# Eight small copy-out tiles instead of six, and an earlier copy-out of the gates' chunk

## The chip, the cores and the metric

The kernel runs on one core of a Trainium2 chip. The metric is the device time of one execution in microseconds (us), the median of several runs. "PE" is the matrix engine, "PEld" its weight load, "DVE" the vector engine, "ACT" the scalar engine, "POOL" GpSimd and "SP" the engine that issues most of the transfers; SPq and POOLq are the instructions by which SP and POOL issue transfers.

## What is computed

One decoder layer on 256 tokens of width 4096, in float32. An RMS norm is followed by one input projection into thirteen groups of columns, by two attention mixers (a dilated one and a sparse one), by gated RMS norms and by an output projection. The part that matters here is the projection:

```python
h = _rmsnorm(x, norm_g[l])
proj = h @ w_in[l]
(q_a, k_a, v_a, z_a, q_b, kc, vc, ksl, vsl, kwn, vwn, z_b, g_b) = jnp.split(
    proj, _split_points(), axis=-1)
```

`q_a`, `k_a`, `v_a` and `q_b` are 2048 columns each, 16 chunks of 512 in all. `g_b` (48 columns) holds the gates of the sparse mixer; the kernel computes it in one chunk with the 256 columns of `vwn`, called `vg` here (304 columns).

## The kernel before, in words

Every operand of a matmul is a sum of a high and a low part in a rounded format (`h` and `l`): ACT rounds the high part, DVE subtracts it from the original and leaves the low part, and each product is three matmuls, h·h, h·l and l·h (`mm3`, L97 to L100). This preparation is called a split.

The program has three stages. In the first, five chunks of the projection are computed from 1 MB pieces of weights; the `vg` chunk is the last of them, and its two sums (one for each half of the tokens) stand in two PSUM banks named `acc`.

The second is the paired stage (`run_pairs`, L409 to L518). Its 16 chunks are taken two at a time: eight groups, in the order q0/q1, k0/k1, v0/v1, qb0/qb1, q2/q3 and so on. A group has 16 steps. A step takes a 2x2 arrangement of weight blocks (two k-tiles by two chunks) and the matching 2x2 arrangement of x blocks. In a **plain** step it does 8 products (24 matmuls), in a **fast** step 7 products (21 matmuls) on sums of blocks; nine steps of a group are fast (`FAST`), seven plain. Before its matmuls a step needs its split (`split_blocks`, L440): for a fast step ACT rounds the raw blocks (L444) and twice sums that DVE has made (L447, L450), while DVE does L445, L448, L449, then the low parts L451 and L452; for a plain step ACT does one rounding of 2048 columns and DVE one subtraction (L105 and L106 of `split_to`). The engines work in the order in which the code is written (`manual_schedule`).

Three operand buffers (`f0`, `f1`, `p`; tiles `bf` and `bp`) hold split operands, and three raw buffers (`bw`) hold loaded weights. `split_on(n)`, called after step n's matmuls, does the splits up to step n+3 whose operand buffer was last used by a step that is done. Each split ends with the load for three steps later (L437 and L438 on SP).

The eight PSUM banks collect eight partial sums, `p1` to `p7` and `e`. The fast steps write p1 to p7; the plain steps write p3, p2, p4 and e. After the last fast step p1, p7, p5 and p6 are final, after the last plain step p3, p2, p4 and e. In groups two to eight the last fast step is two steps before the end, in the first group (order `FIRST`) one step before it. `put_sums` (L462) copies each final bank with ACT into a tile `parts` (128x512, float32) and POOL writes it to the result in HBM: p1 with four plain transfers, the others with accumulating transfers into those of the four result blocks that they belong to (p7 2, p5 2, p6 3, p3, p2, p4 and e one each, 15 transfers in all). Transfers into the same result block follow each other, each waiting until the one before has landed. The `parts` tiles come from a ring of six (L465): the seventh copy of a group (p4) waits until the transfers out of p1's tile have landed, the eighth (e) until those out of p7's have. The next group writes the same eight banks, each as soon as it has been copied.

The copy-out of the last group's p3, p2, p4 and e is left to the third stage's beginning (`rest`), where ACT also rounds that stage's first weights. The third stage does the other projections, both mixers and the output projection.

At the beginning of the paired stage the code loads the weights of three steps, does the splits of steps 0, 1 and 2 (`split_on(-1)`, L485), and then calls `begin` (`begin_pairs`, L1120), which copies the two banks of `vg` out with ACT (`evict_away`, L545, tile `away`) and stores them with SP (L546). The banks of the paired stage are the same memory: step 0 can write the banks under `vg` only after these copies. The order of the first group's steps is plain, plain, fast, plain, fast, fast, plain ...

Of the kernel before, what the change touches and what calls it, by code (L numbers as in the profile page):

```python
# [11 lines left out]
F32 = mybir.dt.float32  # L12
# [6 lines left out]
P = 128  # L19
# [7 lines left out]
CW = 512  # L27
# [56 lines left out]
def hybrid_trunk(ctx: ExitStack, tc: tile.TileContext, a: dict):  # L84
# [9 lines left out]
    room = {}  # L94
# [7 lines left out]
    def split_to(h, l, src, scale=None):  # L102

        if scale is None:
            nc.scalar.activation(h, src, AF.Copy)  # L105
            nc.vector.tensor_sub(l, src, h.bitcast(F32))  # L106
        else:
            nc.scalar.activation(h, src, AF.Copy, scale=scale)
            nc.vector.scalar_tensor_tensor(l, src, scale, h.bitcast(F32), op0=OP.mult, op1=OP.subtract)
# [299 lines left out]
    def run_pairs(dcs, begin):  # L409
# [21 lines left out]
        def load(n):  # L431
            if n < N:
                d, i = steps[n]
                w, (g, half) = raw[n % LOADS], divmod(i, 2)
                ks = slice(2 * half, 2 * half + 2)
                c0, c1 = dcs[d][0]
                nc.sync.dma_start(w[:, B11 : B21 + 1], a["w_in"][c0, g][:, ks])  # L437
                nc.sync.dma_start(w[:, B12 : B22 + 1], a["w_in"][c1, g][:, ks])  # L438

        def split_blocks(n):  # L440
            w, t = raw[n % LOADS], sums_b
            h, l = hl[place[n]][:, 0], hl[place[n]][:, 1]
            if FAST[steps[n][1]]:
                nc.scalar.activation(h[:, :3], w[:, B22:], AF.Copy)  # L444
                nc.vector.tensor_tensor(t[:, T3 : T1 + 1], w[:, B22 : B11 + 1],  # L445
                                        w[:, B12 : B12 + 1].to_broadcast([P, 2, CW]), op=OP.subtract)
                nc.scalar.activation(h[:, 3:5], t[:, T3 : T1 + 1], AF.Copy)  # L447
                nc.vector.tensor_add(t[:, T2], w[:, B22], t[:, T1])  # L448
                nc.vector.tensor_sub(t[:, T4], w[:, B21], t[:, T2])  # L449
                nc.scalar.activation(h[:, 5:], t[:, T2:], AF.Copy)  # L450
                nc.vector.tensor_sub(l[:, :3], w[:, B22:], h[:, :3].bitcast(F32))  # L451
                nc.vector.tensor_sub(l[:, 3:], t, h[:, 3:].bitcast(F32))  # L452
            else:
                split_to(h[:, :4], l[:, :4], w)
            load(n + LOADS)
# [6 lines left out]
        def put_sums(d, ps, banks):  # L462
            dst = [scratch(dcs[d][1][c])[:, m] for c, m in ((0, 0), (1, 0), (0, 1), (1, 1))]
            for b in banks:
                t = room["parts"].tile([P, CW], F32, name="parts", tag="parts", bufs=6)  # L465
                nc.scalar.activation(t, ps[b], AF.Copy)
                for c in {"p1": (0, 1, 2, 3), "p5": (1, 3), "p6": (1, 2, 3), "p7": (2, 3),
                          "p2": (0,), "p3": (1,), "p4": (2,), "e": (3,)}[b]:
                    if b == "p1":
                        nc.gpsimd.dma_start(dst[c], t)  # L470
                    else:
                        nc.gpsimd.dma_start(dst[c], t, accum_op=OP.add)

        split = 0

        def split_on(n):

            nonlocal split
            while split < N and split <= n + 3 and prev[split] <= n:
                split_blocks(split)  # L480
                split += 1

        for n in range(LOADS):
            load(n)
        split_on(-1)  # L485
        begin()
        for n, (d, i) in enumerate(steps):
            if n % NKP == 0:
                ps = {b: room["banks"].tile([P, CW], F32, name=b) for b in BANKS} if d == 0 else dict(ps)
# [7 lines left out]
            if FAST[i]:  # L497
                s = lambda j: (sops[i][:, 0, j], sops[i][:, 1, j])
                e = not any(FAST[k] for _, k in steps[n + 1 : n - n % NKP + NKP])
                raws, sums = -B22, 3  # L500
                for bank, lhs, b in (
                    ("p1", block(i, 0, 0), raws + B11), ("p7", s(2), sums + T3), ("p5", s(0), sums + T1),
                    ("p6", s(1), sums + T2), ("p3", s(3), raws + B22), ("p2", block(i, 0, 1), raws + B21),
                    ("p4", block(i, 1, 1), sums + T4),
                ):
                    product(bank, lhs, b, e and bank in ("p1", "p5", "p6", "p7"))
                if e:
                    put_sums(d, ps, ("p1", "p7", "p5", "p6"))
            else:
                e = n % NKP == NKP - 1  # L510
                for bank, row, cols in (("p3", 0, (B12, B22)), ("p2", 0, (B11, B21)), ("p4", 1, (B11, B21)), ("e", 1, (B12, B22))):
                    for col, b in enumerate(cols):
                        product(bank, block(i, row, col), b, e and col == 1)
                if e and d == len(dcs) - 1:
                    return lambda: put_sums(d, ps, ("p3", "p2", "p4", "e"))
                if e:
                    put_sums(d, ps, ("p3", "p2", "p4", "e"))
# [12 lines left out]
    def scratch(key, width=CW):  # L530
        if key not in scr:
            scr[key] = dram.tile([P, NT, width], F32, name=f"scr_{key}")
        return scr[key]
# [598 lines left out]
    with tc.manual_schedule():  # L1132
        rest = run_pairs(dcs, begin_pairs)
# [85 lines left out]
```

## Time and profile before

| | us |
|---|---|
| median of 3 runs | 1724.02 (1720.05 to 1729.22) |
| the profiled execution, its own time | 1725.84 |
| its span, first to last instruction | 1724.1 |
| paired stage within it | 193.3 to 907.1 |
| PE busy | 1659.7 (96%) |
| DVE busy | 1243.6 (72%) |
| ACT busy | 959.4 (56%) |
| mean granted PE clock | 0.984 |

Rows of the timeline read: start, duration, engine, line and operation, out <- in, count, and in brackets the idle time of the engine before it and what ended that. Rows of the windows read: stretch, its length, and for each engine its busy time and in brackets its instructions, then granted clock as a share of full speed, DMA share and GB/s.

### The profile page before, as it was taken

What the parts mean: (1) busy time and instruction counts of PE and PEld (TensorE: products, weight loads), DVE (VectorE), ACT (ScalarE), POOL (GpSimd) and SP (SyncE); (2) the same over time, 40 slices, a digit from 0 to 9 for tenths busy, and PEclk for the clock granted to TensorE, in tenths of its full rate; (3) what the DMA queues carried; (4) which work ended last, traced back from release to release, by engine and by line L of the source; (5) the groups of instructions that cost most, each with busy time, mean ns of one, the idle gap of its engine ahead of it and who ended that gap; (6) DMA issues with size and microseconds to landing.
All of it is one profiled execution on the core that took longest, in us unless ns stands there. A gap on an engine that the chain in (4) does not pass through costs nothing.

```text
span 1724.1 us, 20835 instructions
## 1 busy us (share of the span) xinstructions
PE 1659.7 (96%) x7853; PEld 1359.1 (79%) x7853; DVE 1243.6 (72%) x1576; ACT 959.4 (56%) x1243; POOL 97.2 (6%) x129
## 2 busy tenths in 40 slices
PE   9999997999999998999998999999999999999997
PEld 6889875787878786878787778777888888888887
DVE  7496596979798887888876778887865655555553
ACT  6676464546465555555545677677654544444443
POOL 0000001011111111020211000000000000000000
PEclk9999998999999899999999999999999999999999
DMA  9875667878787868696969645543454466566554
GB/s 344 297 274 174 202 207 194 243 244 230 245 228 242 238 225 234 224 253 211 269 243 327 239 171 200 199 140 124 158 193 176 169 214 214 213 214 213 202 196 157
DMA packets 92661, 376.74 MB, mean 219 GB/s; under 512 B 10896, under 2 KB 12304, under 8 KB 73104
## 3 DMA queue, kind: packets, MB, share of 16 engines
q1 hardware_dynamic: 73152, 336.61, 55.6%
q0 software_dynamic: 15232, 31.46, 9.5%
q10 hardware_dynamic: 4176, 7.34, 1.3%
q8 instruction: 61, 1.00, 0.2%
q14 instruction: 40, 0.33, 0.1%
HBM read 335.48 MB, written 39.90 MB: 218 GB/s over the span
## 4 chain that ended last, share of the span: by engine, by line
PE 59%; DVE 9%; DMA 9%; issue 6%; ACT 4%; POOL 1%; ACTq 0%; SPq 0%; POOLq 0%; DVEq 0%
PE acc L100 11%; PE acc L99 11%; PE acc L98 11%; PE p L99 6%; PE p L100 5%; PE p L98 5%; DVE bf L452 2%; DMA scr_q<-parts 2%; DMA scr_qb<-parts 2%; DMA bw<-in_w_in 2%; DMA scr_k<-parts 2%; DVE bf L451 2%; DVE bt L445 1%; DMA scr_v<-parts 1%; DVE bt L448 1%
## 5 line engine op out<-in xcount | busy, mean ns | idle before, releaser
L106 DVE TENSOR_TENSOR wl<-w,wh 128x1024 fp32r<-128x1024 f32 (+2 forms) x306 | 365.1, 1194 | 274.4 <-ACT wh L105 273.8
L105 ACT ACTIVATE wh<-w 128x1024 fp32r<-128x1024 f32 (+2 forms) x306 | 316.4, 1035 | 297.0 <-PE acc L100 290.6
L98 PE MATMUL acc<-wh,xh 128*128 128x512 f32 (+2 forms) x768 | 292.5, 382 | 0.5 <-ACT wh L105 0.5
L99 PE MATMUL acc<-wl,xh 128*128 128x512 f32 (+2 forms) x768 | 291.1, 379 | 1.7 <-DVE wl L106 1.6
L100 PE MATMUL acc<-wh,xl 128*128 128x512 f32 (+2 forms) x768 | 291.2, 379 | 0.0
L98 PE MATMUL acc<-wh,yh 128*128 128x512 f32 (+1 forms) x512 | 192.8, 377 | 0.0
L100 PE MATMUL acc<-wh,yl 128*128 128x512 f32 (+1 forms) x512 | 192.5, 376 | 0.0
L99 PE MATMUL acc<-wl,yh 128*128 128x512 f32 (+1 forms) x512 | 192.4, 376 | 0.0
L99 PEld LDWEIGHTS acc<-wl,xh 128*128 128x128 f32 x768 | 144.9, 189 | 26.5 <-DVE wl L106 3.5
L452 DVE TENSOR_TENSOR bf<-bt,bf 128x2048 fp32r<-128x2048 f32 x72 | 164.5, 2285 | 0.8
L98 PEld LDWEIGHTS acc<-wh,xh 128*128 128x128 f32 x768 | 144.7, 189 | 25.4 <-ACT wh L105 2.3
L100 PEld LDWEIGHTS acc<-wh,xl 128*128 128x128 f32 x768 | 144.8, 189 | 24.2
L451 DVE TENSOR_TENSOR bf<-bw,bf 128x1536 fp32r<-128x1536 f32 x72 | 126.1, 1752 | 44.8 <-ACT bf L444 44.8
L106 DVE TENSOR_TENSOR bp<-bw,bp 128x2048 fp32r<-128x2048 f32 x48 | 109.9, 2289 | 62.0 <-ACT bp L105 62.0
L447 ACT ACTIVATE bf<-bt 128x1024 fp32r<-128x1024 f32 x72 | 76.4, 1061 | 140.4 <-DVE bt L445 140.4
L99 PE MATMUL p<-bf,sum 128*128 128x512 f32 x288 | 117.8, 409 | 13.3 <-DVE bf L452 13.2
L105 ACT ACTIVATE bp<-bw 128x2048 fp32r<-128x2048 f32 x48 | 91.6, 1908 | 62.2 <-PE e L100 43.1
L98 PE MATMUL p<-bp,xh 128*128 128x512 f32 x288 | 113.4, 394 | 6.7 <-ACT bp L105 6.7
L444 ACT ACTIVATE bf<-bw 128x1536 fp32r<-128x1536 f32 x72 | 106.6, 1481 | 21.2 <-DMA bw<-in_w_in 19.8
L100 PE MATMUL p<-bf,sum 128*128 128x512 f32 x288 | 114.7, 398 | 0.0
L99 PE MATMUL p<-bp,xh 128*128 128x512 f32 x288 | 113.2, 393 | 1.5 <-DVE bp L106 1.5
L98 PE MATMUL p<-bf,sum 128*128 128x512 f32 x288 | 114.5, 398 | 0.0
(279 smaller groups left out, 2928.4 us busy)
## 6 DMA issues: line engine op xcount, KB each, us to landing
bw<-in_w_in SPq DMA_DIRECT2D x256, 512.0 KB, 5.2
w<-in_w_in SPq DMA_DIRECT2D x76, 1024.0 KB, 4.9
w<-in_w_out SPq DMA_DIRECT2D x64, 1024.0 KB, 4.8
scr_q<-parts POOLq DMA_DIRECT2D x30, 256.0 KB, 7.3
scr_k<-parts POOLq DMA_DIRECT2D x30, 256.0 KB, 8.1
scr_v<-parts POOLq DMA_DIRECT2D x30, 256.0 KB, 8.0
scr_qb<-parts POOLq DMA_DIRECT2D x30, 256.0 KB, 8.7
w<-in_w_vg SPq DMA_DIRECT2D x8, 608.0 KB, 3.7
```

Of the source, the lines that this page charges most:

```text
L98: nc.tensor.matmul(out, lh, rh, start=start, stop=False)
L99: nc.tensor.matmul(out, lh, rl, start=False, stop=False)
L100: nc.tensor.matmul(out, ll, rh, start=False, stop=stop)
L105: nc.scalar.activation(h, src, AF.Copy)
L106: nc.vector.tensor_sub(l, src, h.bitcast(F32))
L444: nc.scalar.activation(h[:, :3], w[:, B22:], AF.Copy)
L445: nc.vector.tensor_tensor(t[:, T3 : T1 + 1], w[:, B22 : B11 + 1], w[:, B12 : B12 + 1].to_broadcast([P, 2, CW]), op=OP.subtract)
L447: nc.scalar.activation(h[:, 3:5], t[:, T3 : T1 + 1], AF.Copy)
L448: nc.vector.tensor_add(t[:, T2], w[:, B22], t[:, T1])
L451: nc.vector.tensor_sub(l[:, :3], w[:, B22:], h[:, :3].bitcast(F32))
L452: nc.vector.tensor_sub(l[:, 3:], t, h[:, 3:].bitcast(F32))
```

## The change

```diff
-                t = room["parts"].tile([P, CW], F32, name="parts", tag="parts", bufs=6)
+                t = room["parts"].tile([P, CW], F32, name="parts", tag="parts", bufs=8)
...
-        split_on(-1)
+        for split in range(2):
+            split_blocks(split)
+        split = 2
         begin()
+        split_on(-1)
```

The ring of copy-out tiles has eight places instead of six, one for each bank of a group. At the beginning of the paired stage the splits of steps 0 and 1 are done first, then `begin`, then the split of step 2. The changed program has three lines more from there on, so that L545 is L548 in it.

ACT at the beginning of the paired stage: `bf` and `bp` are the operand buffers, `away` the copies of the `vg` banks (`acc`). The piece shows the instructions before, with -, and now, with +.

```order
 L105 ACTIVATE bf_1811<-bw_1813 128x2048 [waits DMAHW4_49,DMAHW3_49]
 L105 ACTIVATE bp<-bw_1814 128x2048 [waits DMAHW6_49,DMAHW5_49,DVE_49]
-L444 ACTIVATE bf_1817<-bw_1815 128x1536 [waits DMAHW7_49,DMAHW0_49,PE_49]
+L548 ACTIVATE away<-acc 128x304 [waits PE_49] x2
+L444 ACTIVATE bf_1817<-bw_1815 128x1536 [waits DMAHW7_49,DMAHW0_49]
 L447 ACTIVATE bf_1817<-bt 128x1024 [waits DVE_49]
 L450 ACTIVATE bf_1817<-bt 128x1024 [waits DVE_49]
-L545 ACTIVATE away<-acc 128x304 x2
```

The two copies have moved ahead of the three roundings of step 2's split; they wait for PE (the last matmuls of `vg`) by themselves now.

ACT at the end of the first group: the copies of p3, p2, p4 and e into `parts`, and the next split, of a plain step. DMASW are the semaphores of POOL's transfers.

```order
 L466 ACTIVATE parts<-p_1863 128x512 [waits PE_49]
 L466 ACTIVATE parts<-p_1862 128x512 [waits PE_49]
-L466 ACTIVATE parts<-p_1860 128x512 [waits DMASW1_49,DMASW2_49,DMASW0_49,DMASW3_49,PE_49,Activation_49]
-L466 ACTIVATE parts<-e 128x512 [waits DMASW4_49,DMASW5_49,PE_49,Activation_49]
-L105 ACTIVATE bp<-bw_1815 128x2048 [waits DMAHW7_49,DMAHW6_49]
+L466 ACTIVATE parts<-p_1860 128x512 [waits PE_49]
+L466 ACTIVATE parts<-e 128x512 [waits PE_49]
+L105 ACTIVATE bp<-bw_1815 128x2048 [waits DMAHW7_49,DMAHW6_49,Activation_49]
```

Nothing has moved here; the seventh and the eighth copy no longer wait for transfers.

ACT at the end of the second group, the same four copies and the next split, of a fast step:

```order
-L466 ACTIVATE parts<-p_1863 128x512 [waits DMASW5_49,PE_49]
-L466 ACTIVATE parts<-p_1862 128x512 [waits DMASW6_49,PE_49]
-L466 ACTIVATE parts<-p_1860 128x512 [waits DMASW1_49,DMASW2_49,DMASW0_49,DMASW7_49,PE_49,Activation_49]
-L466 ACTIVATE parts<-e 128x512 [waits DMASW3_49,DMASW4_49,PE_49,Activation_49]
-L444 ACTIVATE bf_1817<-bw_1814 128x1536 [waits DMAHW1_49,DMAHW0_49]
+L466 ACTIVATE parts<-p_1863 128x512 [waits DMASW3_49,PE_49]
+L466 ACTIVATE parts<-p_1862 128x512 [waits DMASW4_49,PE_49]
+L466 ACTIVATE parts<-p_1860 128x512 [waits DMASW5_49,PE_49]
+L466 ACTIVATE parts<-e 128x512 [waits DMASW6_49,PE_49]
+L444 ACTIVATE bf_1817<-bw_1814 128x1536 [waits DMAHW1_49,DMAHW0_49,Activation_49]
```

Here too the order stays; each copy waits for the transfers out of the same bank's tile of the group before, no longer for transfers of its own group. PE's, DVE's and POOL's instructions stand in the same order as before in the whole program. On SP the store of `vg` stands one load earlier, ahead of the load for step 5 that ends step 2's split.

More of the change, by code (lines that the diff above doesn't have):

```diff
@@ L484, in run_pairs @@
             load(n)
+        for split in range(2):
+            split_blocks(split)
+        split = 2
+        begin()
         split_on(-1)
-        begin()
         for n, (d, i) in enumerate(steps):
```

## The prediction

> **What bounds the kernel now.** I read the instructions of the tile `parts` first: who waited for it. A copy into `parts` that waits, waits here for transfers out of an older tile.
>
> ```profile
>   ACT parts L466: 71.8, 13
> ```
>
> ACT stood still for 71.8 us, 13 times, ahead of these copies. ACT is no bottleneck, so this counts only where PE is late after it. The windows, cut where PE starts each group, tell how long a group takes:
>
> ```profile
> 193.30:282.56 89.26, 84.35 (x359) 67.72 (x358) 77.61 (x57) 47.79 (x43) 2.36 (x4) 0.98 0.61 202
> 282.56:378.83 96.27, 84.96 (x358) 68.10 (x357) 75.56 (x53) 50.61 (x43) 12.63 (x16) 0.93 0.77 224
> 378.83:466.07 87.24, 83.02 (x359) 66.40 (x357) 73.39 (x53) 48.84 (x43) 11.39 (x15) 1.00 0.80 238
> 821.06:907.06 86.00, 82.68 (x358) 66.27 (x356) 65.55 (x47) 44.02 (x40) 13.29 (x17) 1.00 0.83 254
> sum 713.76, PE 674.09 PEld 541.38 DVE 587.17 ACT 386.26 POOL 86.97; mean PE 84.26 PEld 67.67 DVE 73.40 ACT 48.28 POOL 10.87
> ```
>
> What could PE do without waits? Two rows of its timeline at the second group's end stand 29 matmuls apart:
>
> ```profile
> 372.04 0.39 PE L98 MATMUL e<-bp,xh 128*128 128x512 f32 x1
> 378.61 0.39 PE L100 MATMUL e<-bf,xl 128*128 128x512 f32 x1
> ```
>
> 6.57/29 = 0.2266 us each. A group has 9x21 + 7x24 = 357 matmuls, so 80.9 us. Eight groups would take 647; they take 713.8. Some 66 us are lost: 8.4 in the first group, 15.4 in the second, and 528.2 - 6x80.9 = 42.8 in the last six (528.2 is the sum less the first two). DVE, with 73 to 78 us of work in a group, is the next engine, close behind PE; ACT has 51 at most.
>
> **The copies, first boundary.** ACT, then DVE and PE:
>
> ```profile
> 278.95 3.02 ACT L466 ACTIVATE parts<-p 128x512 f32<-128x512 f32 x6
> 288.80 0.60 ACT L466 ACTIVATE parts<-p 128x512 f32<-128x512 f32 x1 [6.82 <-DMA scr_q<-parts]
> 294.81 0.60 ACT L466 ACTIVATE parts<-e 128x512 f32<-128x512 f32 x1 [5.42 <-DMA scr_q<-parts]
> 295.31 1.90 ACT L105 ACTIVATE bp<-bw 128x2048 fp32r<-128x2048 f32 x1
> ...
> 297.24 2.29 DVE L106 TENSOR_TENSOR bp<-bw,bp 128x2048 fp32r<-128x2048 f32 x1 [15.50 <-ACT bp L105]
> ...
> 282.33 0.39 PE L100 MATMUL e<-bp,xl 128*128 128x512 f32 x1
> 289.45 0.50 PE L98 MATMUL p<-bf,xh 128*128 128x512 f32 x1 [2.64 <-ACT parts L466]
> 297.26 0.80 PE L98 MATMUL p<-bp,xh 128*128 128x512 f32 x1 [6.74 <-ACT bp L105]
> ```
>
> Six copies run together, the seventh waits 6.82 us and the eighth 5.42. Behind them in ACT's queue stand the roundings of the next splits, and behind these DVE, idle for 15.50 us. PE first waits for p4's bank (2.64), then for the operand (6.74). With eight tiles the seventh copy starts at 281.97. The eighth must still wait for e's last matmul, which ends at 282.33 + 0.39 = 282.72; the copy ends at 283.3, and the rounding of `bp` starts there instead of at 295.31: **12.0 us earlier**, and with it DVE, which from there on sets the pace. The other 3.4 us of this group's 15.4 I leave as lost: DVE enters the group without a lead, as it did in the first.
>
> **The copies, later boundaries.** At the second:
>
> ```profile
> 376.70 1.07 ACT L466 ACTIVATE parts<-p 128x512 f32<-128x512 f32 x2
> 378.89 0.60 ACT L466 ACTIVATE parts<-p 128x512 f32<-128x512 f32 x1 [1.13 <-PE e L99]
> 387.44 0.60 ACT L466 ACTIVATE parts<-e 128x512 f32<-128x512 f32 x1 [7.94 <-DMA scr_k<-parts]
> 387.93 1.48 ACT L444 ACTIVATE bf<-bw 128x1536 fp32r<-128x1536 f32 x1
> ...
> 389.44 1.76 DVE L451 TENSOR_TENSOR bf<-bw,bf 128x1536 fp32r<-128x1536 f32 x1 [6.67 <-ACT bf L444]
> 391.33 2.29 DVE L452 TENSOR_TENSOR bf<-bt,bf 128x2048 fp32r<-128x2048 f32 x1
> ...
> 388.09 0.50 PE L98 MATMUL e<-bp,xh 128*128 128x512 f32 x1 [0.25 <-ACT parts L466]
> ```
>
> PE hardly waits for the bank here (0.25); the cost is DVE's 6.67 us, since the split of the group's third step ends at 391.33 + 2.29 = 393.6. After the change e's copy needs only the group's last matmul (378.61 + 0.39 = 379.0) and ends at 379.6; DVE goes on at 389.44 - 6.67 = 382.8 and is done at 386.9. PE runs one fast and one plain step from 378.83, 45 matmuls, to 389.0, and finds the operand there. So the wait leaves the path. What is late next is DVE in the pairs of fast steps that follow; I leave 1.5 us lost in each of these six groups, between nothing and the 2.8 that the first group lost to the splits' pace alone (8.4 less the 5.6 below). 42.8 - 6x1.5 = **33.8 us**.
>
> The two more tiles cost no instruction. No copy waits for the group before either: a group's last transfer is issued at
>
> ```profile
> 403.15 0.86 POOL L472 DMA_DIRECT2D scr_k<-parts  x1 [0.53 <-issue]
> ```
>
> and the next copies come after 450. POOL's chain (each accumulation waits for the one before into the same block) is bounded by the first six copies as before, so p4's and e's transfers, last in its queue, start no earlier than POOL reaches them.
>
> **The gates' chunk.**
>
> ```profile
> 195.23 1.49 ACT L444 ACTIVATE bf<-bw 128x1536 fp32r<-128x1536 f32 x1 [2.41 <-DMA bw<-in_w_in]
> 199.13 0.72 ACT L545 ACTIVATE away<-acc 128x304 f32<-128x304 f32 x2
> 210.06 1.92 ACT L105 ACTIVATE bp<-bw 128x2048 fp32r<-128x2048 f32 x1 [10.22 <-issue]
> ...
> 193.34 0.40 PE L98 MATMUL p<-bf,xh 128*128 128x512 f32 x1
> 199.90 0.50 PE L98 MATMUL p<-bf,xh 128*128 128x512 f32 x1 [3.65 <-ACT away L545]
> 209.59 0.39 PE L100 MATMUL e<-bp,xl 128*128 128x512 f32 x1
> ...
> 212.01 2.29 DVE L106 TENSOR_TENSOR bp<-bw,bp 128x2048 fp32r<-128x2048 f32 x1 [10.01 <-ACT bp L105]
> ```
>
> The sums of `vg` are final when PE turns to the paired stage at 193.34, but ACT copies them at 199.13, behind step 2's three roundings. Now it copies them from about 193.6 to 194.4. Queued behind is only step 2's L444, whose weights land at 195.23, so the added wait for PE delays nothing. SP's store of `vg` can go at 194.4 too and holds up no load: the one behind it waits for DVE's part of step 2's split. PE no longer waits. Its first two steps, 48 matmuls, would end at 193.34 + 10.9 = 204.2; they end at 209.59 + 0.23 = 209.8. Step 3's operand buffer comes free then, ACT starts at 210.06, DVE at 212.01, and DVE works without a pause from there. So all of it comes **5.6 us earlier**: 3.65 of wait, the rest in matmuls that ran slowly after it.
>
> The Trainium skill, in "TensorE: Matmul & The Clock Gate", section "What's actually happening", says that after an idle window of about 3.4 us the array runs at half clock until it has been busy for about as long. By that rule the slow part would be worth an estimated 1.7 us and the term 5.4 instead of 5.6; the trace agrees.
>
> **The third stage's start.**
>
> ```profile
> 906.44 2.94 ACT L105 ACTIVATE wh<-w 128x1024 fp32r<-128x1024 f32 x3
> 914.32 0.60 ACT L466 ACTIVATE parts<-e 128x512 f32<-128x512 f32 x1 [4.95 <-DMA scr_qb<-parts]
> 919.69 0.44 PE L792 MATMUL ph<-w1hl,bhl 128*60 128x256 f32 x1 [3.88 <-ACT w1hl L105]
> ```
>
> e's copy waited 4.95 us and PE stood 3.88 us behind it. Between nothing (the transfers are dense there and may be late next) and 4.95, I take **3.7 us**, near PE's own wait.
>
> **Sum.** 5.6 + 12.0 + 33.8 + 3.7 = 55.1 us off the profiled execution's 1725.84, hence 1670.7. The median is 1.8 lower: **1669 us**.
>
> **The rivals.**
>
> *The transfers take it back.* Taking the stalls out presses the same bytes into less time.
>
> ```profile
> q1 hardware_dynamic: 73152, 336.61, 55.6%
> q0 software_dynamic: 15232, 31.46, 9.5%
> ...
> bw<-in_w_in SPq DMA_DIRECT2D x8, 512.0 KB, 7.7
> bw<-in_w_in SPq DMA_DIRECT2D x22, 512.0 KB, 4.9
> ```
>
> The last two rows are the weights' loads at 365 to 380 us, beside POOL's transfers, and at 395 to 450. A group's 16.8 MB take 16.8/336.61 x 0.556 x 1724 = 47.8 us of the 16 engines, POOL's transfers an eighth of 0.095 x 1724, 20.5 us: 68 of 80.9. That is for the average; near a boundary a load takes half as long again, and three raw buffers may not cover it. If half of 12.0 + 33.8 is lost to late loads, 23 us, the time is 1692. The skill's "DMA: Bandwidth & Descriptors", section "Queues, rings and completion order", has each engine alternate between queues packet by packet; the 7.7 against 4.9 agrees.
>
> *The copies wait on.* If the seventh and eighth copy still end where they did (the ring's places not being what they wait for), only the 5.6 us of the start go: 1718, no measurable change. The order of instructions, in which those waits are gone, speaks against it.
>
> *Slower: the clock.* If PE at work without pauses were granted a lower clock in the paired stage, its 647 us would stretch. From 0.91 on the stage is as long as now (647/713.8); at 0.88 it takes 735, and with the 3.7 at the end the time is 1742.
>
> ```profile
> 940.00:1724.00 784.00, 766.12 (x3884) 635.24 (x3882) 505.15 (x947) 426.62 (x694) 2.51 (x4) 1.00 0.54 190
> ```
>
> Against it: 766 busy us of 784 at clock 1.00. The second group's 0.93 comes with waits, not with load.
>
> **How the numbers follow.** Forecast 0.79, late loads 0.13, waits that stay 0.05, the clock 0.03. The forecast by itself reaches from all 66 us of the stage gone and 4.95 at the end (71 off the median: 1653) to 1684 (4 us lost in each later group). With the late loads' 1692 the range is 1653 to 1692. A measurement of this kernel can tell some 0.5% (8.6 us) from no change: faster 0.92, same 0.05, slower 0.03.
>
> **What would show it.** In the changed profile: no ACT wait for a `scr` transfer ahead of L466; the 3.65 us behind `away` gone; groups of about 82 us, the second about 84; DVE's idle time ahead of L451 at the boundaries gone; clock near 1.00. The forecast is wrong if groups still take 86 or more, and the ACT and DVE waits for `bw` (late loads) say whether the transfers did it.

## The result, and the profile after

| | us |
|---|---|
| after, median of 4 runs | 1668.49 (1666.68 to 1669.00) |
| before, median of 4 runs beside them | 1724.16 (1720.05 to 1729.22) |
| after / before | 0.9674, 95% interval 0.9647 to 0.9701 |
| the profiled execution after: its own time, its span | 1669.0, 1667.2 |
| paired stage, before and after | 713.8, 655.0 |
| third stage (to the end of the span), before and after | 817.0, 818.9 |

The change takes 55.7 us off, 3.3%; the forecast was 1669. The sum over two traces hides that one term came out larger and another not at all, so the profile is read by terms here.

First the waits of ACT, in which the copies' waits for transfers had stood (what waits, what for; us in total, times, longest):

```profile
ACT bf L444 <- DMA bw<-in_w_in: 35.3, 25, 3.5
...
ACT parts L466 <- PE p L100: 7.4, 3, 5.9
...
ACT parts L466 <- PE e L100: 4.0, 7, 0.8
```

No copy into `parts` waits for a transfer any more, only for the sum itself. The waits for weights have grown (35.3 us; the same row was 19.8, 16 times, before): the same loads have to come in less time.

The windows, cut as before where PE starts each group (stretch, length, busy time and instructions of PE, PEld, DVE, ACT, POOL, then PE's granted clock, DMA share, GB/s):

```profile
193.39:277.30 83.91, 82.69 (x361) 66.83 (x359) 77.84 (x57) 48.41 (x44) 2.37 (x4) 1.00 0.65 215
277.30:361.35 84.05, 82.54 (x358) 66.48 (x357) 75.78 (x53) 50.74 (x43) 12.67 (x16) 1.00 0.85 257
361.35:442.29 80.94, 80.94 (x359) 66.93 (x358) 73.24 (x53) 48.99 (x42) 11.70 (x15) 1.00 0.84 258
...
767.42:848.35 80.93, 80.93 (x358) 66.74 (x356) 65.27 (x47) 44.55 (x39) 13.50 (x17) 1.00 0.86 271
sum 654.96, PE 651.48 PEld 534.53 DVE 586.69 ACT 388.49 POOL 87.15; mean PE 81.44 PEld 66.82 DVE 73.34 ACT 48.56 POOL 10.89
```

From the third group on a group takes nearly what its 357 matmuls take, 80.9: the six have 80.9 to 81.8. In the first two groups 3 us each are still lost. DVE's work in a group is as before; its waits for ACT ahead of L451, 44.8 us in six waits before, have no row any more.

The timeline at the three places of the change (start, duration, instruction, and in brackets the idle time before it):

```profile
193.39 0.85 ACT L548 ACTIVATE away<-acc 128x304 f32<-128x304 f32 x2 [0.29 <-PE acc L100]
195.78 1.50 ACT L444 ACTIVATE bf<-bw 128x1536 fp32r<-128x1536 f32 x1 [1.53 <-DMA bw<-in_w_in]
204.80 1.92 ACT L105 ACTIVATE bp<-bw 128x2048 fp32r<-128x2048 f32 x1 [5.24 <-PE e L100]
...
273.70 3.50 ACT L466 ACTIVATE parts<-p 128x512 f32<-128x512 f32 x7
277.50 0.60 ACT L466 ACTIVATE parts<-e 128x512 f32<-128x512 f32 x1 [0.30 <-PE e L100]
277.99 1.91 ACT L105 ACTIVATE bp<-bw 128x2048 fp32r<-128x2048 f32 x1
...
850.52 0.59 ACT L466 ACTIVATE parts<-e 128x512 f32<-128x512 f32 x1
...
882.11 2.00 ACT L105 ACTIVATE w1hl<-w 128x1024 fp32r<-128x1024 f32 x2 [3.68 <-DMA w<-in_cmp_v_w]
...
885.26 0.39 PE L98 MATMUL pk<-hh,w2h 128*128 128x30 f32 x1 [3.52 <-ACT hh L105]
```

At the start `away` is copied at 193.39, step 2's rounding behind it waits for its weights anyway, and step 3's begins at 204.80 where it began at 210.06. At the first boundary seven copies run together, e's follows e's last matmul by 0.3 us, and the rounding of `bp` starts at 277.99, right behind. At the third stage's beginning e's copy doesn't wait either; but 30 us later ACT waits 3.68 us for weights, and PE stands 3.52 us behind it. That stall was not there before: the one ahead of `ph` was, of 3.88 us.

### The profile page after: what moved, and what is told of

Same layout as the page of the kernel before. It is cut to its first block, busy times and chain, and to the rows that moved or that the text cites. A ratio compares the mean times of both kernels' runs of the same rounds, so it can differ in the third digit from the quotient of the medians.

```text
span 1667.2 us, 20825 instructions
## 1 busy us (share of the span) xinstructions
PE 1638.6 (98%) x7853; PEld 1354.0 (81%) x7853; DVE 1243.7 (75%) x1576; ACT 961.7 (58%) x1243; POOL 97.4 (6%) x129
## 3 DMA queue, kind: packets, MB, share of 16 engines
q0 software_dynamic: 15232, 31.46, 9.1%
## 4 chain that ended last, share of the span: by engine, by line
PE 78%; DVE 9%; DMA 6%; issue 3%; ACT 3%; SPq 0%; ACTq 0%; POOLq 0%; POOL 0%; DVEq 0%
PE acc L100 15%; PE acc L99 15%; PE acc L98 15%; PE p L99 8%; PE p L100 8%; PE p L98 8%; DMA bw<-in_w_in 4%; DVE bf L452 2%; DVE bf L451 2%; DVE bt L445 1%; PE e L100 1%; PE e L99 1%; PE e L98 1%; DMA w<-in_cmp_v_w 1%; DVE wl L106 1%
## 5 line engine op out<-in xcount | busy, mean ns | idle before, releaser
L444 ACT ACTIVATE bf<-bw 128x1536 fp32r<-128x1536 f32 x72 | 106.9, 1485 | 44.7 <-DMA bw<-in_w_in 35.3
L451 DVE TENSOR_TENSOR bf<-bw,bf 128x1536 fp32r<-128x1536 f32 x72 | 126.1, 1751 | 0.0
L99 PE MATMUL p<-bf,sum 128*128 128x512 f32 x288 | 113.3, 393 | 3.5 <-DVE bf L452 3.4
L100 PE MATMUL p<-bf,sum 128*128 128x512 f32 x288 | 112.2, 390 | 0.0
L98 PE MATMUL p<-bf,sum 128*128 128x512 f32 x288 | 112.2, 389 | 0.0
L99 PE MATMUL p<-bp,xh 128*128 128x512 f32 x288 | 112.1, 389 | 0.0
L100 PE MATMUL p<-bp,xl 128*128 128x512 f32 x288 | 112.0, 389 | 0.0
```

Of the source, the lines that this page charges most:

```text
L98: nc.tensor.matmul(out, lh, rh, start=start, stop=False)
L99: nc.tensor.matmul(out, lh, rl, start=False, stop=False)
L100: nc.tensor.matmul(out, ll, rh, start=False, stop=stop)
```

## The experiments

The theory: with eight places the copies' waits leave the path, at every boundary and at the third stage; DVE then has a lead that covers the rest. The rivals: the transfers take part of it back, and parts of the gain come from elsewhere. Edits are against the changed kernel, if nothing else is said. Times stand beside runs of the kernel before on the same chip, whose medians were 1725.47, 1724.28, 1725.54 and 1724.28 us in the four sets of runs; the changed kernel, run once more, had 1667.60 (1667.29 to 1668.33), ratio 0.967 (0.9657 to 0.9683).

> The changed kernel unaltered, as the measure for the runs beside it: 1668 us.

Its groups ended within 1.1 us of those above, and its PE stood 3.8 us at the same place in the third stage.

### Each part alone

The gates' part alone (the ring at six):

```diff
-name="parts", tag="parts", bufs=8)
+name="parts", tag="parts", bufs=6)
```

> The earlier copy-out of the gates' chunk alone, with six copy-out tiles. My theory: it gives what PE and DVE gained at the beginning of the paired stage in the two traces, 5.3 us, and nothing else, since the next boundary's waits take their own time afterwards: 1719 us (1717 to 1721). Rival: a gain ahead of the first boundary is swallowed there, because the copies wait for transfers; then 1724, no change.

Measured: 1719.92 (1717.07 to 1723.69), ratio 0.9971 (0.9959 to 0.9982).

The ring alone (the kernel before, with `bufs=8`):

> Eight copy-out tiles alone, the gates' chunk copied as before. My theory: the two parts add up, so it is slower than the changed kernel by the beginning's 5.3 us: 1674 us (1672 to 1676), with PE's 3.65 us of waiting for the copies of the gates' chunk still there. Rival: the parts overlap, and the ring alone gives nearly all, 1669.

Measured: 1673.24 (1671.53 to 1676.09), ratio 0.9706 (0.9687 to 0.9725). PE's wait at the start is still in its timeline:

```profile
199.86 0.80 PE L98 MATMUL p<-bf,xh 128*128 128x512 f32 x1 [3.65 <-ACT away L545]
```

5.6 and 52.2 us: together 57.8, where both at once gave 55.7 and 56.7. So the parts nearly add up, and the first is near its forecast of 5.6, though its interval reaches from 3.1 to 7.1 us. Most of the other experiments are on the ring's 52.

### Seven places

```diff
-name="parts", tag="parts", bufs=8)
+name="parts", tag="parts", bufs=7)
```

> The changed kernel with seven copy-out tiles: only the eighth copy of a group waits, for the four plain transfers out of its own group's first tile. My theory: what counts is the age of those transfers. At the later boundaries they were issued 11 us before and have landed, so nothing is lost; at the first boundary they are issued 3 us before, the copy waits some 6 to 7 us and DVE with it: 1675 us (1672 to 1678). Rival: each missing tile costs about half of the ring's gain at every boundary: 1692 or more.

Measured: 1672.95 (1671.83 to 1674.16), ratio 0.9702 (0.9683 to 0.972). With seven tiles e's copy takes p1's tile of its own group. In later groups p1 is copied two steps ahead, and its transfers have mostly landed by then: the row of the tile `parts` (who waited for it, us, times) has two waits in the whole program. That row, the timeline at the first boundary, and the windows of the second to fourth group:

```profile
  ACT parts L466: 7.2, 2
```

```profile
273.70 3.51 ACT L466 ACTIVATE parts<-p 128x512 f32<-128x512 f32 x7
283.56 0.60 ACT L466 ACTIVATE parts<-e 128x512 f32<-128x512 f32 x1 [6.35 <-DMA scr_q<-parts]
```

```profile
277.09:367.16 90.07, 84.47 (x360) 68.78 (x359) 75.53 (x53) 50.79 (x44) 12.50 (x16) 0.96 0.81 240
367.16:448.09 80.93, 80.93 (x359) 66.94 (x357) 73.42 (x53) 49.06 (x42) 12.13 (x17) 1.00 0.83 258
448.09:529.02 80.93, 80.93 (x358) 66.95 (x357) 73.12 (x53) 48.94 (x42) 10.91 (x15) 1.00 0.84 256
```

One wait of 6.35 us costs its group 6.0 us (90.07 against 84.05). A wait at the first boundary, where DVE has no lead, is paid nearly in full. The next two groups are at 80.93 again: the loss does not carry on.

### Is DVE's lead the cover?

```diff
-                nc.scalar.activation(t, ps[b], AF.Copy)
+                for _ in range(4 if b == "e" else 1):
+                    nc.scalar.activation(t, ps[b], AF.Copy)
```

e's copy is made four times, so ACT has some 1.9 us more at each boundary, ahead of the next split.

> The changed kernel with the copy of bank e done four times instead of once, which holds ACT 1.5 us longer at each group's end, ahead of the next splits. My theory: at the later boundaries the splits have a lead of some 1.5 us over PE and cover it, so it costs about 1.5 at the first boundary and little at the others: 1671 us (1670 to 1674). Rival, the forecast's view that DVE enters each group with hardly any lead: 1.5 us at each of seven boundaries, 1679.

Measured: 1671.68 (1669.37 to 1671.83), ratio 0.9691 (0.9673 to 0.9709). The copies at the first boundary, and the windows of the second and third group:

```profile
277.43 2.49 ACT L467 ACTIVATE parts<-e 128x512 f32<-128x512 f32 x4 [0.30 <-PE e L100]
```

```profile
277.23:363.23 86.00, 82.78 (x359) 66.47 (x358) 75.51 (x53) 52.41 (x46) 12.79 (x17) 1.00 0.84 251
363.23:444.36 81.13, 81.13 (x359) 66.87 (x358) 73.18 (x53) 50.26 (x45) 10.74 (x15) 1.00 0.84 256
```

The delay is paid in full once, at the first boundary (86.00 against 84.05). The last six groups lose 1.4 us together (488.4 against 487.0), of six times 1.9 us added. DVE has 73 us of work in a group of 81, so it can gain over 7 us on PE in each group and come to the next boundary ahead.

### The transfers, in the paired stage

All accumulating transfers of the first seven groups are made twice, the second time into blocks that nothing reads (in the first group these second ones are plain):

```diff
                         nc.gpsimd.dma_start(dst[c], t, accum_op=OP.add)
+                        twice = scratch(f"twice_{b}{c}")[:, 0]
+                        if d == 0:
+                            nc.gpsimd.dma_start(twice, t)
+                        elif d < len(dcs) - 1:
+                            nc.gpsimd.dma_start(twice, t, accum_op=OP.add)
```

> The changed kernel with every accumulating transfer of the first seven groups done a second time into blocks of its own that nobody reads. My theory: the transfers are next to bound the paired stage; a group's transfers, 68 us of all engines' time, grow by about 15 to 83, more than PE's 80.9, and near each boundary loads come late beyond what the splits' lead covers: 3 to 6 us in each of seven groups, 1690 to 1710 us. Rival: three raw buffers and the lead cover it as they cover the present late loads: 1668 to 1672.

Measured: 1666.63 (1665.43 to 1669.14), ratio 0.9664 (0.9647 to 0.9681). I had expected a loss of 20 us and more; there is none. The page's row of POOL's queue (packets, MB, share of the 16 engines over the span; 31.46 MB and 9.1% in the changed kernel), the waits of ACT, and a window of the third group:

```profile
q0 software_dynamic: 25616, 51.65, 15.2%
```

```profile
ACT bf L444 <- DMA bw<-in_w_in: 90.9, 44, 3.3
```

```profile
360.99:441.94 80.95, 80.95 (x359) 66.95 (x358) 73.35 (x53) 48.94 (x42) 20.52 (x27) 1.00 1.00 292
```

The engines are full now in the third group (DMA share 1.00 instead of 0.84), and ACT waits 90.9 us for late weights instead of 35.3. The groups take what they took. Late loads come, but ACT waits at most 3.3 us for one, and the lead covers them, as the rival said.

### The transfers, at the third stage

e's copy lost its wait of 4.95 us there, and the third stage got no shorter. Four experiments ask why. In the first the copies p4 and e of the last group go into the tiles of p1 and p7, so that the wait is back in this group alone:

```diff
+        kept = {}
...
+                if d == len(dcs) - 1 and b in ("p4", "e"):
+                    t = kept["p1" if b == "p4" else "p7"]
+                else:
+                    t = kept[b] = room["parts"].tile([P, CW], F32, name="parts", tag="parts", bufs=8)
```

> The changed kernel in which, in the last group alone, the copies of p4 and e go into the tiles of p1 and p7 again, so that they wait for transfers as before the change. My theory: the third stage's beginning is bound by the transfers, and the wait of e's copy stands beside that, so nothing is lost: 1668 us (1667 to 1670), with PE waiting behind e's copy again and no longer for the compression's weights later. Rival, the forecast's term for the third stage: 3.7 us are lost, 1672.

Measured: 1664.76 (1663.98 to 1669.18), ratio 0.9657 (0.9639 to 0.9676).

```profile
853.37 0.60 ACT L471 ACTIVATE parts<-e 128x512 f32<-128x512 f32 x1 [4.87 <-DMA scr_qb<-parts]
858.73 0.30 PE L800 MATMUL ph<-w1hl,bhl 128*60 128x256 f32 x1 [3.79 <-ACT w1hl L105]
...
883.98 0.28 PE L98 MATMUL pk<-hh,w2h 128*128 128x30 f32 x1 [0.38 <-ACT hh L105]
```

The wait is back, with PE's stall of 3.79 us behind it, and the time is no longer. The late stall has shrunk from 3.52 to 0.38. So the stall only changes its place; the forecast's gain of 3.7 us is refuted. That this kernel is even 3 us below the changed one is explained in part. Of the 2.8 us between its span, 1663.0, and the 1665.8 of the changed kernel's second trace, 1.7 lie in the third stage: PE's granted clock fell to 0.50 behind the stall in both, for 3.41 us here and for 6.83 us there, and 3.41 us at half clock are some 1.7 us of PE's work. The rest stays open, and the runs of the two touch.

Two edits moved the loads instead. One set the pace at which the third stage's tasks are mixed into its first chunk of matmuls to 1.0 and raised it from 1.45 to 1.525 for the later ones (`pace=1.0 if n == 0 else 1.525`); the other loads the mask constants later, behind the second `compress` task, on top of the other order of the first group that is shown further down:

> The changed kernel with the third stage's mixer tasks advanced less often beside its first chunk of weights (pace 1.0) and a little more often later (1.525 instead of 1.45). My theory: the compression's weights then come over a longer stretch, the transfers no longer run full, and the 3.5 us stall goes: 1664 to 1666 us. Rival: the tasks put off are missing at the end, where PE then waits for the mixers: 1670 or more.

Measured: 1668.34 (1667.66 to 1669.38), ratio 0.9673 (0.966 to 0.9687).

```profile
886.70 0.28 PE L98 MATMUL pk<-hh,w2h 128*128 128x30 f32 x1 [3.19 <-ACT hh L105]
```

> The other order of the first group together with a later load of the mask constants (0.8 MB) at the third stage's beginning. My theory: 0.8 MB fewer ahead of the compression's first weights is 2.4 us of transfers at 335 GB/s, of which one or two reach PE: 1662 to 1663 us beside the 1664 of the order alone. Rival: the constants only move within the same full stretch, and the time stays at 1664.

Measured: 1664.32 (1662.35 to 1667.35), ratio 0.9651 (0.9633 to 0.9668), nothing gained on the order alone.

```profile
864.71 0.47 PE L795 MATMUL ph<-w1hl,bhl 128*60 128x256 f32 x1 [4.81 <-ACT w1hl L105]
```

Both failed in the same way: the stall stays (3.19 us) or moves (4.81), and neither run is clearly faster.

Then the last group's eleven accumulating transfers were left out (`elif d < len(dcs) - 1:` in place of `else:`; four result blocks are then incomplete):

> The changed kernel without the eleven accumulating transfers of the last group, so that the result blocks of that group stay incomplete; all other work is the same. My theory: the third stage's first 45 us are bound by the transfers, so with 2.9 MB of them and their accumulation gone the 3.5 us stall of PE behind the compression's weights goes, and the third stage takes 814 us or less instead of 818.9: 1663 us (1661 to 1665). Rival: the compression's own chain over ACT, DVE and PE sets the time there, and nothing changes: 1668.

Measured: 1659.43 (1658.99 to 1660.24), ratio 0.9622 (0.9609 to 0.9635). Below what was expected; so the transfers cost more than the visible stall. Last, they were replaced by plain transfers of the same tiles, one behind the other into blocks that nothing reads (the result blocks are as incomplete as without them):

```diff
+                    elif d == len(dcs) - 1:
+                        nc.gpsimd.dma_start(scratch(f"plain_{c}")[:, 0], t)
```

> The last group's eleven accumulating transfers write the same bytes from the same tiles, each waiting for the one before as now, but as plain transfers into blocks that nothing reads, so nothing is read back and added (four result blocks lack seven of their eight sums, so their values are incomplete). Leaving these transfers out altogether gave 1659.4. If the reading back and adding is what holds the transfer engines at the third stage's beginning, this comes near that: 1659 to 1662. If it is the bytes written beside the loads, it stays near the changed kernel: 1666 to 1669. About 1664 would mean half each.

Measured: 1659.51 (1658.37 to 1660.27), ratio 0.9623 (0.9608 to 0.9638). The first 50 us of the third stage, in the kernel before, the changed one, the one without the transfers and the one with plain ones:

```profile
907.06:957.06 50.00, 44.48 (x224) 35.60 (x224) 35.20 (x46) 28.75 (x37) 6.86 (x8) 0.93 1.03 334
```

```profile
848.35:898.35 50.00, 44.17 (x222) 35.62 (x222) 36.55 (x47) 29.35 (x37) 6.87 (x8) 0.93 1.03 335
```

```profile
846.90:896.90 50.00, 48.61 (x266) 38.84 (x266) 41.68 (x52) 34.31 (x42) 0.00 (x0) 1.00 0.81 317
```

```profile
846.47:896.47 50.00, 48.73 (x267) 39.20 (x267) 42.04 (x52) 34.62 (x42) 2.20 (x5) 1.00 0.91 365
```

Before and after PE does the same in these 50 us, 224 and 222 matmuls, wherever its stall lies. Without the accumulating transfers it does 266, and with plain ones 267. The clock tells how a stall of 3.5 us can cost more than 8: the 0.93 of the changed kernel is a clock of 0.50 for 6.83 us from 884.30 on, behind the stall, some 3.4 us of PE's work, and without the stall the clock is 1.00. The two together are most of the difference. The DMA engines' queues in the same 50 us (packets, MB, share of the 16 engines; q1 are the loads, q0 POOL's transfers), first of the changed kernel, then with plain transfers:

```profile
q1 hardware_dynamic: 2511, 13.85, 71.1%
q0 software_dynamic: 1579, 2.87, 31.7%
```

```profile
q1 hardware_dynamic: 2884, 16.09, 80.1%
q0 software_dynamic: 640, 2.10, 10.4%
```

A MB of accumulating transfers took 11.0% of the engines in 550 packets, a MB of plain ones 5.0% in 305, so a packet took a quarter more as well. Beside them 13.85 MB of loads came in, against 16.09. (The 2.10 MB are eight of the eleven plain transfers; the others had run before.) It isn't the bytes written but the accumulating that holds the third stage up, by some 8.5 us: from where PE turns to the third stage to the end it takes 818.9 us in the changed kernel, 810.3 in these two.

The Trainium skill, in "DMA: Bandwidth & Descriptors", section "Queues, rings and completion order", has each engine take turns between its queues, a packet at a time. The measured shares fit that: more packets on q0 are more turns taken from the loads.

### Another order of the first group

What is still lost in the paired stage is 3 us in each of the first two groups. In the changed `FIRST` one fast step of the last pair has moved to the fourth place, so that DVE has work early:

```diff
-FIRST = [0, 0, 1, 0, 1, 1, 0, 1, 1, 0, 1, 1, 0, 1, 1, 0]
+FIRST = [0, 0, 1, 1, 0, 1, 1, 0, 1, 1, 0, 1, 1, 0, 1, 0]
```

> The changed kernel with another order of the first group's steps: plain, plain, fast, fast, plain and so on, with plain, fast, plain at its end. My theory: the 3 us that the first and the second group still lose come from splits that have no lead, since the first group's third split waits for step 1's buffer and its end is fast, fast, plain; with this order both groups take about 81.5 us: 1664 us (1662 to 1666). Rival: late loads or the accumulations cost these 3 us, and the order changes nothing: 1668.

Measured: 1664.11 (1663.17 to 1665.72), ratio 0.9649 (0.9636 to 0.9663), below every run of the changed kernel, and so faster than both. The windows of the second and third group:

```profile
274.24:359.13 84.89, 82.75 (x359) 66.42 (x358) 76.18 (x54) 52.04 (x46) 13.79 (x19) 1.00 0.87 259
359.13:440.08 80.95, 80.95 (x359) 66.97 (x357) 73.21 (x53) 49.05 (x42) 11.52 (x15) 1.00 0.84 257
```

The second group now starts at 274.24 instead of 277.30, so the first group's loss is gone; the second's stays (84.89 - 80.9 = 4.0), though the expectation had both gone. So the time came out as expected in part by luck. Between this span, 1661.4, and the 1665.8 of the changed kernel's second trace, 1.7 of the 4.4 us were gained up to the end of the paired stage, and 2.7 in the third stage, where PE ran at half clock for 3.41 us instead of 6.83.

## Why the prediction was right, step by step

| term | predicted | measured in the two traces |
|---|---|---|
| the gates' chunk | 5.6 | 5.3 |
| first boundary (second group) | 12.0 | 96.27 - 84.05 = 12.2 |
| the last six groups | 33.8 | 41.2 |
| the third stage's start | 3.7 | 817.0 - 818.9 = -1.8 |
| sum | 55.1 | 56.9 |

**The gates' chunk** is right in size and cause: 5.3 in the trace, 5.6 by the runs with this part alone.

**The first boundary** is right. The rounding came at 277.99, right behind e's copy, as worked out, and 3.1 us of the group's 15.4 stayed, where 3.4 were left as lost. The runs with seven tiles and with the longer copy show the cause: what ACT is late there, PE pays.

**The last six groups**: the mechanism was right, the term mis-sized by 7.4 us. The step that failed is "I leave 1.5 us lost in each of these six groups": they lost 0.3 each (654.96 - 83.91 - 84.05 = 487.0, less 6x80.9: 1.6 in all). I took the first group's 2.8 for the upper bound and a value between it and nothing. But that loss comes of starting without a lead, and from the second boundary on there is one: with 1.9 us added at each boundary the third group lost 0.2 more.

**The third stage's start** was wrong, the step "I take 3.7 us, near PE's own wait". The wait was real and it went, but the transfer engines were full there, and what the copy no longer waited for, a load did 30 us later. The other end of that term, "nothing (the transfers are dense there and may be late next)", was the right one. Putting the wait back cost nothing; taking the accumulating out gave 8.5 us.

The two misses, +7.4 and -5.5, nearly cancel, so it is luck that the total came closer than its terms. (DVE's "73 to 78 us of work in a group" leaves out the last group, whose row shows 65.55; no term rests on that.)

**The rivals.** "The transfers take it back" was wrong for the paired stage, to which it was priced: doubled accumulating transfers cost nothing there. My working, 68 of 80.9 us of the engines' time, made a queue's share of the engines an amount of work that must fit in; late loads became more and harmed nothing. It holds at the third stage, where DVE and ACT have no such lead. "The copies wait on" is refuted by the waits, and the lower clock by the windows: 1.00 in every group of the changed kernel, 0.93 to 1.00 before.

## What to carry to other kernels

Price a removed wait by who is late behind it and by what lead that engine has there: a wait is paid in full where the lead is nothing (the first boundary) and costs nothing where the engine gains several us per group. Where the transfer engines are full at a place, a wait removed there can come back at a later load, as here; ask which transfers fill them, and in what form, before you move waits about. A ring with one place for each tile of a group made the copies independent of the transfers; one place less cost 6 us, at one boundary only.

## What the runs showed of the hardware

**An accumulating transfer costs the engines about twice a plain one**, per MB, in the 50 us measured above (11.0% against 5.0%, with transfers of 256 KB beside the loads). Whether the last group's sums can be collected in another way without giving that gain back wasn't tried.

**The short waits cost more than their length.** PE's timeline in the kernel before, in the fifth group:

```profile
565.40 0.50 PE L98 MATMUL e<-bp,xh 128*128 128x512 f32 x1 [2.37 <-ACT parts L466]
...
566.71 0.63 PE L100 MATMUL e<-bp,xl 128*128 128x512 f32 x1
567.13 0.63 PE L98 MATMUL p<-bf,xh 128*128 128x512 f32 x1
568.57 0.80 PE L99 MATMUL p<-bf,xh 128*128 128x512 f32 x1 [0.81 <-DVE bf L451]
...
570.99 0.80 PE L99 MATMUL p<-bf,sum 128*128 128x512 f32 x1 [0.77 <-DVE bf L452]
571.58 0.63 PE L100 MATMUL p<-bf,sum 128*128 128x512 f32 x1
...
576.70 0.47 PE L100 MATMUL p<-bf,xl 128*128 128x512 f32 x1
577.01 0.40 PE L98 MATMUL p<-bf,xh 128*128 128x512 f32 x1
```

From 566.71 to 576.70 most matmuls follow each other at 0.43 us instead of 0.23, and the granted clock is 0.50 from 566.61 to 576.85. In the paired stage before, PE stood idle 25 times, 39.5 us in all, and 63 matmuls started over 0.40 us behind the one ahead without a wait, which costs 13.8 us more; after the change it is five times, 3.4 us, and one matmul. Nearly a quarter of the 58.8 us that the stage gained was such slow running, which went with the waits.

The Trainium skill, in "TensorE: Matmul & The Clock Gate", section "What's actually happening", puts the half clock behind an idle window of some 3.4 us. Here it began 1.2 us after the wait of 2.37 us had ended, ahead of the other two, and no wait of the three is that long; the measurement decides.

In this trace's paired stage the half clock began six times, always on a grid of 3.41 us, and lasted 3.41, 6.83, 10.24 or 13.65 us. Each time PE had stood 1.9 us or more within the 3.41 us ahead; where it stood 1.7 us or less within such a stretch, the clock stayed full. (The ends of matmuls are modelled, so these lengths are rough.)
